# A hybrid decoder step on one core: four changes of order, among them a third pair of the second feed-forward in plain products

## The chip, the cores and the metric

The kernel runs on one core of a Trainium2 chip. The metric is the device time of one execution in microseconds (us); three runs of the kernel before have a median of 1526.13 us (1524.22 to 1526.34). Lower is better. In the text PE is TensorE, DVE is VectorE, ACT is ScalarE, POOL is GpSimd, SP is SyncE.

## The reference

One layer of a decoder, for 512 prompt tokens with 16 meta tokens ahead of them, and for 32 new tokens of 8 running sequences (560 columns in all, of which the last stages keep 544). The width is 1024, the feed-forward is 2816 wide.

```python
h = x + 0.5 * rms_norm(swiglu(rms_norm(x, ffn1_pre_g), ffn1_w_gate, ffn1_w_up, ffn1_w_down), ffn1_post_g)
u = rms_norm(h, mix_pre_g)
proj = u @ w_in
...
m = jax.nn.sigmoid(gate_a) * (o_a @ w_o_gla) + jax.nn.sigmoid(gate_b) * (o_b @ w_o_sb)
h = h + rms_norm(m @ w_out, mix_post_g)
y = h + 0.5 * rms_norm(swiglu(rms_norm(h, ffn2_pre_g), ffn2_w_gate, ffn2_w_up, ffn2_w_down), ffn2_post_g)
```

with `swiglu(x, g, u, d) = (silu(x @ g) * (x @ u)) @ d`. Between `proj` and `m` lie a gated linear attention (with a decay from a rank-16 projection, `w_gk2`), and a stick-breaking attention over the prompt and over cached pages.

## The kernel before, in words

All activations lie transposed: 128 features on the partitions, tokens along the free axis. Every matrix product is made of three products at a reduced float format (`float32r`): a weight and an activation are each split into a high part (a cast, on ACT) and a low part (value less high part, on DVE), and high x high, high x low and low x high are added in PSUM. One k-tile of one tile of 128 outputs is thus three matmuls for each half of the columns.

The program issues PE, DVE, ACT and POOL in an order that is written out by hand. A loop of matmuls calls `step()` after each k-tile (in the paired products after every two). Work of the other engines is put on a list with `later(n, f)`: f is issued n steps on, at that place of its engine's queue. Some stages have a table of their own besides (`when(n, f)`, n counted in steps of the stage). Each queue runs in order: an operation that waits holds up all that stand behind it. Loads are issued by SP, in order as well; weights land in three buffers (`raw`), and the next load of weights is issued when the low part of an earlier one has been made and its buffer is free.

Four places matter here.

**Gate rows.** In the pass over the value tiles of the mixer, `ranks` (the rank-16 projection) is followed by `ranks_end`, which writes its high and low parts in three row groups with `stack` (L216 to L223: a copy on ACT, two operations on DVE). `gla_gates` (L300s) then puts the pieces of head 0 on the list: `Gates.ranks` (two matmuls at L288 and two activations at L289), logs, sums and exponentials.

**Gates of the mixer.** The list `MIXER` gives the order in which output gates and output products are made: "R" is a plain product of eight k-tiles, "S" a pair of tiles made at once by `seven_steps` (L921 to L923), with seven products of half size where plain ones take eight (a form of Strassen's scheme). Such a pair needs sums of activations. They are made early, stored in DRAM (`sums_dram`) and come back by `sums_back` at the steps of `SUMS_BACK`, two loads (L2082) for each of four indices. Eight and ten steps later `sums_hi` casts them on ACT (L2088), two steps behind each of these `sums_lo` makes the low parts on DVE (L152 is the line of a helper that records every DVE `tensor_tensor`). The first pair begins at step 120 of this stage. In `seven_steps` the accumulator c takes a first product, is read by DVE (`v`, the sum of e5 and c), and then takes its last one.

**Output product.** `m @ w_out` runs tile by tile, for the first half of the columns (n = 0 to 7), then for the second. Its activations are `ms`, eight k-tiles, each made by `mixed` (L2250s) from a product `product_b`: the gate times the product, plus the other branch, then the cast (L2259) and the low part. The eighth is made from the product just ahead. `nm.tile` squares and scales each finished tile (L735, L736).

**Second feed-forward.** `early_tiles` makes the first three pairs of gate and up tiles; `other_tiles` makes the others by a plan, one letter for a pair: "R" is `eight` (L1081 to L1084: 96 matmuls, two tiles of eight k-tiles), "S" is `seven` (L1141 to L1143: 84 matmuls). The first "R" reads the normalised activations of `early_tiles` and 280 and 264 columns; from the second on the scaled copies `ub` are read, 272 and 272. `scaled_h`, `scaled_hi` and `scaled_lo` make `ub` (L1001 is the cast); `summed`, `sums_hi` (L1022) and `sums_lo` make the sums for the seven-product pairs, from the step `SP0` and again `SPE` steps later, (SP0, SPE) = `SUM2`. An "R" takes 16 steps of this stage and an "S" 14. The weights of the second and third plain pair are split by `parted` (the cast at L852) at 5 and at 1 step ahead of their tile; for a seven-product pair `weight_sums` (DVE) begins 10 steps ahead. The first feed-forward runs the same function with `PLAN1`, `SUM1` and 280 columns a half.

Of the kernel before, what the change touches and what calls it, by code (L numbers as in the profile page):

```python
# [17 lines left out]
KD = D // P  # L18
# [12 lines left out]


PLAN1 = "RRRSSSSSSSSSSSSSSSS"
PLAN2 = "RRSSSSSSSSSSSSSSSSS"
LATE1, LATE2 = 8, 8
SUM1, SUM2 = (14, 16), (4, 11)
UP1 = (2, 5)
UP2 = (2, 5)
RE_FFN = 3
U_SUMS = (5, 6, 9)  # L40
KEEP = 5
SUMS_BACK = (80, 86, 92, 106)
MIXER = [("R", "r", n) for n in range(3, 8)]
MIXER += [("R", "o", n) for n in range(8)] + [("R", "a", 0), ("R", "a", 1), ("S", "b", 0), ("S", "a", 2), ("S", "b", 2), ("R", "p", 0), ("R", "p", 1)]
MIXER += [("S", "a", 4), ("R", "p", 2), ("R", "p", 3), ("S", "b", 4), ("S", "a", 6), ("R", "p", 4), ("R", "p", 5), ("S", "b", 6)]
# [75 lines left out]
def hybrid_step(  # L121
# [25 lines left out]
    def ps(tag="ps"):  # L147
        count[0] += 1
        return pp.tile([P, 512], F32, tag=tag, name=f"{tag}{count[0]}")
# [58 lines left out]
    g_mix, g_mixpost, g_pre2 = gains[:, 8:16], gains[:, 16:24], gains[:, 24:32]  # L208
# [37 lines left out]
    W2 = (HW, W1)  # L246
# [68 lines left out]
    def gla_gates(hd, at, by):  # L315
        g = Gates(hd)
        for n, f in enumerate((g.ranks, g.logs, g.sums, g.exps)):
            later(at + by[n], f)
# [366 lines left out]
    def k_steps(acc, parts, k0, k1, kt, act, halves, nw=P, wid=(HW, HW)):  # L685
        hi, lo = parts
        for k in range(k0, k1):
            a = {h: act.get(k, h, wid[h]) for h in halves}
            wh, wl = hi[k - k0], lo[k - k0]
            for h in halves:  # L690
                T.matmul(acc[h][:nw, : wid[h]], wh, a[h][0], start=(k == 0), stop=False)  # L691
                T.matmul(acc[h][:nw, : wid[h]], wh, a[h][1], start=False, stop=False)  # L692
            for h in halves:
                T.matmul(acc[h][:nw, : wid[h]], wl, a[h][0], start=False, stop=(k == kt - 1))  # L694
            step()
# [17 lines left out]
    def later(n, f):  # L713
        todo.append([n, f])
# [498 lines left out]
    st.todo += [(w_out[0], 0, KD, P * n, P, n < 7 and "tile") for n in range(8)]  # L1213
    gate_up_weights(PLAN2, ffn2_w_gate[0], ffn2_w_up[0], 0)
    st.todo += [(ffn2_w_down[0], CUTS[j][0] * P, (CUTS[j][1] - CUTS[j][0]), P * n, P, False) for n, hs, j in by_chunks(DOWN) if (n, hs) != (7, (1,))]
    E = mybir.EngineType
    with tc.manual_schedule(engines={E.PE, E.DVE, E.Activation, E.Pool}):
# [217 lines left out]
        for h in range(2):  # L1435
            ranks(h)
            if h == 0:
                later(LATE[0], lambda: ranks_end(0))
            else:
                later(LATE[1], lambda: ranks_end(1))  # L1440
                gla_gates(0, 24, (0, 4, 7, 13))
                for k in range(KD):
                    later(MIX[0] + MIX[1] * k, lambda k=k: mix_tile(0, k))
                    later(32 + MIX[1] * k, lambda k=k: mix_tile(1, k))
                later(32 + MIX[1] * KD, mix_lo)
            for n in range(6):
                if h == 0:
                    vparts[n] = st.parts.pop(0)
                if h == 0 and n < 5 or h and n in (2, 4):
                    st.split()  # L1450
                    st.fetch()
                if n % 2 == 0:
                    vacc = [{h: ps("acc")} for _ in range(2)]
                for e in range(2):
                    value_chunk(n, e, vacc[e])
                if h and n > 1:
                    give(*vheld[n - 2])
        for n in (6, 7):
            vparts[n] = st.parts.pop(0)
        for e in range(2):  # L1460
            acc = {h: ps("acc") for h in range(2)}
# [14 lines left out]
        for j in range(5):  # L1476
            n = P if j < 4 else NTL
# [32 lines left out]
        for hd, head in enumerate(HEADS):  # L1510
# [10 lines left out]
            for c in range(2):  # L1521
# [3 lines left out]
                while True:  # L1525
                    try:
                        next(g)
                    except StopIteration as e:
                        acc = e.value
# [266 lines left out]
    for c in range(2):  # L1796
        t = cp.tile([P, 16], I32, name=f"idx{c}")
# [220 lines left out]
    def ahead():  # L2018
        st.split()
        st.fetch()  # L2020
# [118 lines left out]
    with tc.manual_schedule(engines={E.PE, E.DVE, E.Activation, E.Pool}):  # L2139
        kps = {}  # L2140
        for pr in range(9):
# [67 lines left out]
            n = 0  # L2209
# [33 lines left out]
        n = 8 * len(PAGES)  # L2243
# [3 lines left out]
        ms, msp = Parts(), {}  # L2247
# [27 lines left out]
        starts, n = {}, 0  # L2275
# [11 lines left out]
        for i in range(4):  # L2287
            when(SUMS_BACK[i], sums_back, i)
            for m in range(2):
# [20 lines left out]
        n = 0  # L2310
# [14 lines left out]
        def product(act, hs, parts):  # L2325
            acc = {h: ps("acc") for h in hs}
            k_steps(acc, parts, 0, KD, KD, act, hs, wid=W2)
            return acc
# [1 line left out]
        u2, rs2 = Parts(), take(NT)  # L2330
        n2 = Gain(u2, g_pre2, rs2, W2)

        nm, held = Norm(g_mixpost, W2), {}
        for i, (n, h) in enumerate([(n, 0) for n in range(8)] + [(n, 1) for n in range(7, -1, -1)]):
            if h == 0 or i % 2:
                ahead()
            if h == 0:
                held[n] = st.parts.pop(0)
            acc = product(ms, (h,), held[n])
            if h and n < 7:  # L2340
                give(*st.rooms[n])
            later(1, lambda n=n, h=h, acc=acc: nm.tile(n, h, acc[h]))
            if (n, h) == (7, 0):
                later(2, exp_ln_table)
            if (n, h) in ((7, 0), (0, 1)):
                for k in range(KD):
                    give(*ms.t[k, h])
                todo.extend([d, f] for d, f in n2.pieces(nm, h, *F1))
        del st.rooms[:7]
        hid, pairs = Parts(), {}  # L2350
        feed2 = other_tiles(u2, g_pre2, rs2, NW, W2, hid, pairs, PLAN2, LATE2, SUM2, UP2)
        early_tiles(u2, rs2, W2, NW, hid, pairs, {(0, 0): 9, (1, 0): 9}, lambda: next(feed2))
# [76 lines left out]
```

## Time and profile before

| | us |
|---|---|
| runs shown, median (lowest to highest) | 1526.13 (1524.22 to 1526.34) |
| the profiled execution | 1520.3 |
| its span, first to last instruction | 1518.6 |
| PE busy | 1499.9 |
| DVE busy | 1044.4 |
| ACT busy | 760.8 |
| mean granted TensorE clock | 0.996 |

The page is of one execution. Its first part gives the time in which each engine ran at least one instruction. A matmul's row lasts about 290 ns, since it counts from its start to its modelled end; the next one starts well before that. In a timeline each row gives the start and the duration in us, the engine, the line, the operation, what it writes and reads, the shapes, how many instructions were merged, and in brackets the idle time of the engine ahead of it with what ended that. In a table of stretches each engine has its busy time and its number of instructions, and the granted clock stands behind.

### The profile page before, as it was taken

What the parts mean: (1) busy time and instruction counts of PE and PEld (TensorE: products, weight loads), DVE (VectorE), ACT (ScalarE), POOL (GpSimd) and SP (SyncE); (2) the same over time, 40 slices, a digit from 0 to 9 for tenths busy, and PEclk for the clock granted to TensorE, in tenths of its full rate; (3) what the DMA queues carried; (4) which work ended last, traced back from release to release, by engine and by line L of the source; (5) the groups of instructions that cost most, each with busy time, mean ns of one, the idle gap of its engine ahead of it and who ended that gap; (6) DMA issues with size and microseconds to landing.
All of it is one profiled execution on the core that took longest, in us unless ns stands there. A gap on an engine that the chain in (4) does not pass through costs nothing.

```text
span 1518.6 us, 29559 instructions
## 1 busy us (share of the span) xinstructions
PE 1499.9 (99%) x11939; PEld 1446.4 (95%) x11939; DVE 1044.4 (69%) x1833; ACT 760.8 (50%) x1396; POOL 150.1 (10%) x216
## 2 busy tenths in 40 slices
PE   8999999999999999999999999999999999999998
PEld 8999999999999889999888999999999999999997
DVE  5788888523777766877776544987577998885234
ACT  6455454424665556566555443534465555444234
POOL 3000000000000111123324551000000000000000
PEclk9999999999999999999999999999999999999999
DMA  7133334524555473334555668335531344333343
GB/s 229 62 98 97 99 97 124 156 78 127 161 136 155 115 112 87 86 81 117 130 104 132 194 197 198 97 100 148 148 115 44 98 120 126 101 116 102 87 116 98
DMA packets 279577, 181.84 MB, mean 120 GB/s; under 512 B 10170, under 2 KB 264432, under 8 KB 279440
## 3 DMA queue, kind: packets, MB, share of 16 engines
q1 hardware_dynamic: 274000, 163.09, 40.5%
q0 software_dynamic: 5440, 16.85, 3.1%
q8 instruction: 94, 1.54, 0.4%
q14 instruction: 43, 0.35, 0.1%
HBM read 157.17 MB, written 22.74 MB: 118 GB/s over the span
## 4 chain that ended last, share of the span: by engine, by line
PE 91%; DVE 4%; ACT 3%; DMA 1%; issue 1%; SPq 0%; DVEq 0%; ACTq 0%
PE acc L691 9%; PE acc L692 9%; PE acc L694 9%; PE acc L1143 8%; PE acc L1141 8%; PE acc L1142 8%; PE acc L678 8%; PE acc L679 7%; PE acc L681 7%; DVE room L152 2%; PE ps L1763 1%; PE acc L921 1%; PE acc L923 1%; PE acc L922 1%; PE ps L1747 1%; PE acc L1084 1%
## 5 line engine op out<-in xcount | busy, mean ns | idle before, releaser
L152 DVE TENSOR_TENSOR lo<-raw,hi 128x1024 fp32r<-128x1024 f32 (+1 forms) x216 | 258.3, 1196 | 169.8 <-ACT hi L657 162.8
L152 DVE TENSOR_TENSOR room<-room,room 128x544 fp32r<-128x544 f32 (+17 forms) x369 | 238.9, 668 | 126.9 <-ACT room L735 57.6
L678 PE MATMUL acc<-room,hi 128*128 128x280 f32 (+1 forms) x928 | 271.7, 310 | 0.1
L1141 PE MATMUL acc<-room,hi 128*128 128x272 f32 (+1 forms) x924 | 267.7, 290 | 0.0
L1143 PE MATMUL acc<-room,lo 128*128 128x272 f32 (+1 forms) x924 | 267.5, 289 | 0.0
L1142 PE MATMUL acc<-room,hi 128*128 128x272 f32 (+1 forms) x924 | 267.5, 289 | 0.0
L679 PE MATMUL acc<-room,hi 128*128 128x280 f32 (+1 forms) x928 | 250.7, 289 | 0.0
L691 PE MATMUL acc<-room,hi 128*128 128x280 f32 (+1 forms) x784 | 221.8, 292 | 0.0
L692 PE MATMUL acc<-room,hi 128*128 128x280 f32 (+1 forms) x784 | 219.0, 289 | 0.0
L657 ACT CAST hi<-raw 128x1024 fp32r<-128x1024 f32 (+1 forms) x130 | 131.8, 1014 | 143.4 <-PE acc L692 124.9
L681 PE MATMUL acc<-room,lo 128*128 128x280 f32 (+1 forms) x928 | 192.6, 289 | 0.0
L694 PE MATMUL acc<-room,lo 128*128 128x280 f32 (+1 forms) x784 | 192.4, 290 | 0.0
L678 PEld LDWEIGHTS acc<-room,hi 128*128 128x128 f32 x928 | 174.9, 188 | 12.6 <-issue 10.7
L679 PEld LDWEIGHTS acc<-room,hi 128*128 128x128 f32 x928 | 175.1, 189 | 2.8 <-issue 1.9
L1143 PEld LDWEIGHTS acc<-room,lo 128*128 128x128 f32 x924 | 173.9, 188 | 0.0
L1141 PEld LDWEIGHTS acc<-room,hi 128*128 128x128 f32 x924 | 173.9, 188 | 0.0
L1142 PEld LDWEIGHTS acc<-room,hi 128*128 128x128 f32 x924 | 173.8, 188 | 0.0
L691 PEld LDWEIGHTS acc<-room,hi 128*128 128x128 f32 x784 | 147.6, 188 | 2.2 <-issue 0.9
L692 PEld LDWEIGHTS acc<-room,hi 128*128 128x128 f32 x784 | 147.5, 188 | 0.2
L852 ACT CAST hi<-raw 128x1024 fp32r<-128x1024 f32 x86 | 90.2, 1053 | 109.5 <-PE acc L1142 51.7
L681 PEld LDWEIGHTS acc<-room,lo 128*128 128x128 f32 x928 | 145.0, 188 | 0.0
L694 PEld LDWEIGHTS acc<-room,lo 128*128 128x128 f32 x784 | 133.9, 188 | 0.0
(354 smaller groups left out, 2831.4 us busy)
## 6 DMA issues: line engine op xcount, KB each, us to landing
raw<-in_w_in_dram SPq DMA_DIRECT2D x49, 512.0 KB, 8.5
raw<-in_ffn_w_down_dram SPq DMA_DIRECT2D x42, 448.0 KB, 3.8
raw<-in_ffn_w_gate_dram SPq DMA_DIRECT2D x66, 256.0 KB, 3.0
raw<-in_ffn_w_up_dram SPq DMA_DIRECT2D x66, 256.0 KB, 3.1
raw<-in_ffn_w_down_dram SPq DMA_DIRECT2D x21, 512.0 KB, 4.1
out_dram<-room SPq DMA_DIRECT2D x32, 256.0 KB, 3.0
raw<-in_w_in_dram SPq DMA_DIRECT2D x28, 256.0 KB, 4.4
h_dram<-room SPq DMA_DIRECT2D x24, 280.0 KB, 3.4
```

Of the source, the lines that this page charges most:

```text
L152: (eng or V).tensor_tensor(out=out, in0=a, in1=b, op=op)
L657: S.copy(h_, src)
L678: T.matmul(acc[h][:, : wid[h]], hi[k], a[h][0], start=(k == 0), stop=False)
L679: T.matmul(acc[h][:, : wid[h]], hi[k], a[h][1], start=False, stop=False)
L681: T.matmul(acc[h][:, : wid[h]], lo[k], a[h][0], start=False, stop=(k == KD - 1))
L691: T.matmul(acc[h][:nw, : wid[h]], wh, a[h][0], start=(k == 0), stop=False)
L692: T.matmul(acc[h][:nw, : wid[h]], wh, a[h][1], start=False, stop=False)
L694: T.matmul(acc[h][:nw, : wid[h]], wl, a[h][0], start=False, stop=(k == kt - 1))
L852: S.copy(hi[:, :kt], src)
L1141: T.matmul(x[:, :QW], hi, act[k][0], start=(first and k == 0), stop=False, skip_group_check=True)
L1142: T.matmul(x[:, :QW], hi, act[k][1], start=False, stop=False, skip_group_check=True)
L1143: T.matmul(x[:, :QW], lo, act[k][0], start=False, stop=(k == 3), skip_group_check=True)
```

## The change

Four edits. `PLAN2` makes the third pair of `other_tiles` in the second feed-forward a plain one ("R" for "S") and `SUM2` puts its sums at steps 14 and 30 where they stood at 4 and 15, so that the second plan and its sums are those of the first. The last entry of `SUMS_BACK` goes from 106 to 102. The pieces of the gate of head 0 begin 27 steps behind the ranks, not 24. And the output product makes seven k-tiles of tile 0, seven of tile 1, and then the eighth of both; `nm.tile` of both follows there.

```diff
-PLAN2 = "RRSSSSSSSSSSSSSSSSS"
+PLAN2 = "RRRSSSSSSSSSSSSSSSS"
 LATE1, LATE2 = 8, 8
-SUM1, SUM2 = (14, 16), (4, 11)
+SUM1, SUM2 = (14, 16), (14, 16)
...
-SUMS_BACK = (80, 86, 92, 106)
+SUMS_BACK = (80, 86, 92, 102)
...
-                gla_gates(0, 24, (0, 4, 7, 13))
+                gla_gates(0, 27, (0, 4, 7, 13))
...
-        nm, held = Norm(g_mixpost, W2), {}
+        nm, held, begun_ = Norm(g_mixpost, W2), {}, {}
         for i, (n, h) in enumerate([(n, 0) for n in range(8)] + [(n, 1) for n in range(7, -1, -1)]):
             if h == 0 or i % 2:
                 ahead()
             if h == 0:
                 held[n] = st.parts.pop(0)
+            if h == 0 and n < 2:
+                begun_[n] = {0: ps("acc")}
+                k_steps(begun_[n], held[n], 0, KD - 1, KD, ms, (0,), wid=W2)
+                if n:
+                    for m, acc in begun_.items():
+                        k_steps(acc, [t[KD - 1 :] for t in held[m]], KD - 1, KD, KD, ms, (0,), wid=W2)
+                        later(1, lambda m=m, acc=acc: nm.tile(m, 0, acc[0]))
+                continue
             acc = product(ms, (h,), held[n])
```

ACT's queue in the second feed-forward, where the weights of its second pair are cast: before. L852 casts the weights (`hi` from `raw`), L1022 the sums, L1088 is the activation of the first plain pair.

```order
L1001 COPY room_64_10597<-room_81_13221 128x544
L835 COPY room_36_3329<-room_40_5185 128x544
L1022 COPY room_78_12783<-room_82_13254 128x544
L1022 COPY room_68_11084<-room_82_13254 128x544
L1088 ACTIVATE room_80_13122<-room_80_13122 128x544
L1022 COPY room_84_13318<-room_83_13255 128x544 x2
L852 COPY hi_13322<-raw_12786 128x1024
L852 COPY hi_13357<-raw_13142 128x1024
```

The same place of ACT's queue in the change:

```order
L1001 COPY room_58_8967<-room_83_13222 128x544
L835 COPY room_37_4493<-room_33_962 128x544
L1088 ACTIVATE room_82_13173<-room_82_13173 128x544
L852 COPY hi_13311<-raw_12788 128x1024
L852 COPY hi_13344<-raw_13143 128x1024
L835 COPY room_58_8967<-room_82_13173 128x544
L1022 COPY room_80_12785<-room_84_13336 128x544
L1022 COPY room_78_12569<-room_84_13336 128x544
```

Four casts of sums stood ahead of the two weight casts and now stand behind them. On DVE, six operations for the sums (four of `summed`, two low parts) stood ahead of the weight's low part and stand behind it.

DVE's queue ahead of the first seven-product pair of the gates, before. The first row is the last of the weight sums, `room_40_5185` times `room_67` is a gate times its product, `lo` is a weight's low part, the rows that write `room_37` and `room_20` are the low parts of the last sums, L1994 copies small pieces of the sampled tokens.

```order
L152 TENSOR_TENSOR room_44_5335<-raw_10662,room_44_5335 128x512
L152 TENSOR_TENSOR room_40_5185<-room_67_10774,room_40_5185 128x544
L152 TENSOR_TENSOR lo_10803<-raw_10578,hi_10802 128x1024
L152 TENSOR_TENSOR room_37_4493<-room_33_962,room_66_10680 128x544
L1994 COPY room_40_5185<-ps_10813 64x32 x2
L1994 COPY room_43_5306<-ps_10813 64x32 x2
L1994 COPY room_5_70<-ps_10813 64x32 x2
L1994 COPY room_38_4495<-ps_10813 64x32 x2
L152 TENSOR_TENSOR room_20_260<-room_33_962,room_20_260 128x544
```

And in the change:

```order
L152 TENSOR_TENSOR room_44_5335<-raw_10662,room_44_5335 128x512
L152 TENSOR_TENSOR room_37_4493<-room_40_5185,room_66_10680 128x544
L152 TENSOR_TENSOR room_20_260<-room_33_962,room_20_260 128x544
L152 TENSOR_TENSOR room_40_5185<-room_67_10775,room_40_5185 128x544
L152 TENSOR_TENSOR lo_10806<-raw_10578,hi_10805 128x1024
L1994 COPY room_40_5185<-ps_10816 64x32 x2
```

The two low parts went ahead of the gate's product and of the weight's low part.

PE's queue in the output product, before, from the seventh k-tile of tile 0 (`acc_12261`) to the first of tile 1 (`acc_12299`). `room_31_874` holds the eighth k-tile of `ms`.

```order
L691 MATMUL acc_12261<-room_62_10030,room_63_10527 128x280
L692 MATMUL acc_12261<-room_63_10527 128x280
L694 MATMUL acc_12261<-room_62_10030,room_64_10597 128x280
L691 MATMUL acc_12261<-room_31_874,room_63_10527 128x280
L692 MATMUL acc_12261<-room_31_874,room_63_10527 128x280
L694 MATMUL acc_12261<-room_31_874,room_64_10597 128x280
L691 MATMUL acc_12299<-room_70_11346,room_64_10597 128x280
```

In the change, from the seventh k-tile of tile 1 (`acc_12297`) to the end of both; the eighth k-tile is in `room_14_144`, and tile 0 is `acc_12262`.

```order
L691 MATMUL acc_12297<-room_62_10030,room_66_10680 128x280
L692 MATMUL acc_12297<-room_64_10597,room_66_10680 128x280
L694 MATMUL acc_12297<-room_62_10030,room_66_10680 128x280
L691 MATMUL acc_12262<-room_14_144,room_64_10597 128x280
L692 MATMUL acc_12262<-room_14_144,room_64_10597 128x280
L694 MATMUL acc_12262<-room_14_144,room_65_10612 128x280
L691 MATMUL acc_12297<-room_14_144,room_66_10680 128x280
```

The 21 matmuls of tile 1's first seven k-tiles now stand ahead of the first matmul that reads the eighth.

## The prediction, made before the changed kernel ran

> **What bounds the kernel now.** I read the page first, then the waits of TensorE, then the timeline and the stretches around the four places that the change touches. The page's span and busy lines come first:
>
> ```profile
> span 1518.6 us, 29559 instructions
> PE 1499.9 (99%) x11939; PEld 1446.4 (95%) x11939; DVE 1044.4 (69%) x1833; ACT 760.8 (50%) x1396; POOL 150.1 (10%) x216
> ```
>
> TensorE (PE) is busy for 99% of the span. A change can gain only by fewer matmuls or by shorter pauses of PE. The two longest waits of PE at one place, with total, times and longest:
>
> ```profile
> PE ps L2364 <- DVE room L152: 3.2, 1, 3.2
> PE acc L1081 <- ACT hi L852: 2.3, 1, 2.3
> ```
>
> The first is the kernel's tail, which the change leaves alone. The second is in the second feed-forward, one of the four seams. To price a pause I need what a matmul costs in the stream, which is not its own duration (about 290 ns, since matmuls overlap) but its pitch. Three stretches of PE; the columns are us, busy time (instructions), granted clock, DMA share, GB/s:
>
> ```profile
> 1175.00:1177.50 2.50, 0.21 (x2) 1.00 0.00 0
> 1177.50:1181.00 3.50, 3.23 (x12) 0.51 0.19 45
> 1210.00:1360.00 150.00, 150.00 (x1199) 1.00 0.38 112
> ```
>
> The third stretch is the steady second feed-forward: 150 us over 1199 matmuls, **0.125 us a matmul**. The second is the cost that the wait list does not show: behind the pause the granted clock is 0.51, and 12 matmuls take 3.46 us (from 1177.54 to 1181.00) where 1.50 would do. All losses below are start to start, less 0.125 for each matmul.
>
> **Seam 1, gate rows three steps later.** PE, then DVE, before:
>
> ```profile
> 440.91 0.29 PE L288 MATMUL ps<-room,wgk 128*128 128x280 f32 x1
> 442.01 0.37 PE L288 MATMUL ps<-room,wgk 128*128 128x280 f32 x1 [0.81 <-DVE room L221]
> 442.22 0.29 PE L691 MATMUL acc<-room,room 128*128 128x280 f32 x1
> ```
> ```profile
> 441.57 0.30 DVE L221 CAST room<-room 16x280 fp32r<-16x280 f32 x1
> ```
>
> The two gate matmuls take 1.31 us from 440.91 to 442.22 instead of 0.25: **1.06 lost**. The second waits for the copy that ends at 441.87. The change puts nine value matmuls ahead of the pair, 9 x 0.125 = 1.13, so the second is due at 440.91 + 1.13 + 0.13 = 442.17, 0.3 behind the copy. What the step issues besides (two activations, one DVE operation, later the logs, sums and exponentials) goes back by three steps too: the exponentials come at step 40 of the 64 that this pass of value tiles still has, ahead of the first head. I cost that at nothing. If the cover of 0.3 is gone, the price is what is missing of it.
>
> **Seam 2, the last sums loaded four steps earlier.** PE's two pauses, in the first and the second seven-product pair of the gates:
>
> ```profile
> 959.69 0.29 PE L923 MATMUL acc<-room,lo 128*128 128x272 f32 x1
> 960.82 0.39 PE L921 MATMUL acc<-room,hi 128*128 128x272 f32 x1 [0.84 <-DVE room L152]
> 961.05 0.28 PE L922 MATMUL acc<-room,hi 128*128 128x272 f32 x1
> ```
> ```profile
> 971.29 0.29 PE L923 MATMUL acc<-room,lo 128*128 128x272 f32 x1
> 971.77 0.39 PE L921 MATMUL acc<-room,hi 128*128 128x272 f32 x1 [0.19 <-DVE room L152]
> 972.00 0.29 PE L922 MATMUL acc<-room,hi 128*128 128x272 f32 x1
> ```
>
> The first loses 1.36 - 0.25 = 1.11, the second 0.71 - 0.25 = 0.46. What PE waits for is not a sum but DVE's addition `v`, which must read the accumulator before the last product adds to it. DVE runs through from 946.59 to there:
>
> ```profile
> 945.16 0.73 DVE L152 TENSOR_TENSOR room<-room,room 128x544 f32<-128x544 f32 x1 [1.49 <-ACT room L2050]
> 946.59 1.23 DVE L152 TENSOR_TENSOR lo<-raw,hi 128x1024 fp32r<-128x1024 f32 x1 [0.70 <-ACT hi L852]
> ```
> ```profile
> 960.34 0.43 DVE L152 TENSOR_TENSOR room<-room,acc 128x272 f32<-128x272 f32 x1
> ```
>
> The change moves the two low parts of the last sums out of this queue, ahead of the row at 945.16, into its idle 1.49. Each is one 128x544 operation at 0.65 (five in 3.25, in the row at 1174.60 below). So `v` ends 1.3 earlier, at 959.47, and PE wants it at 959.69 + 0.125 = 959.81: the first pause closes by 0.3. In the second pair PE comes 1.11 earlier, and wants its `v` at 971.29 + 0.125 - 1.11 = 970.30; DVE gives it at 971.71 - 1.3 = 970.41. I leave 0.2 there: **gain 1.11 + 0.26 = 1.37**. The loads themselves move past the two quarter loads of the next weights on SyncE's queue:
>
> ```profile
> 928.03 2.65 SPq L2082 DMA_DIRECT2D room<-sums_dram  x1
> 932.90 1.35 SPq L617 DMA_DIRECT2D raw<-in_w_in_dram  x2
> ```
>
> The queue stood empty from 930.68 to 932.90, when the weights' buffer came free; the second load of sums takes this place, so I let the weights land as before. Were they late, DVE's weight sums would be late by as much, and the gain would go first.
>
> **Seam 3, the first two output tiles end with their eighth k-tile.**
>
> ```profile
> 1076.81 0.29 PE L694 MATMUL acc<-room,room 128*128 128x280 f32 x1
> 1077.67 0.40 PE L691 MATMUL acc<-room,room 128*128 128x280 f32 x1 [0.56 <-ACT room L2259]
> 1078.83 0.40 PE L692 MATMUL acc<-room,room 128*128 128x280 f32 x1 [0.76 <-DVE room L152]
> 1079.07 0.29 PE L694 MATMUL acc<-room,room 128*128 128x280 f32 x1
> ```
> ```profile
> 1078.06 0.72 DVE L152 TENSOR_TENSOR room<-room,room 128x544 fp32r<-128x544 f32 x1
> ```
>
> Three matmuls take 2.26: **1.88 lost** to the last mixer tile, whose low part is ready at 1078.78. The change puts 21 matmuls of tile 1 (2.63 us) ahead: the low part is wanted at 1076.94 + 2.63 + 0.125 = 1079.69, 0.9 behind. No matmul is added. The squares and scalings of tile 0 come eight steps later, beside those of tile 1: four ACT operations of 0.4 to 0.5 in a row, behind which weight splits for tiles 4 and on stand; PE comes to tile 4 only after tiles 2 and 3, 48 matmuls or 6 us. Of four accumulators two are open for longer, and tile 4 is the first to ask for one of them again, behind the same 6 us. I cost that at nothing.
>
> **Seam 4, the third pair plain and the sums from step 14.** PE, ACT and DVE where the second pair begins:
>
> ```profile
> 1174.93 0.28 PE L1084 MATMUL acc<-room,lo 128*128 128x264 f32 x1
> 1177.54 0.59 PE L1081 MATMUL acc<-room,hi 128*128 128x272 f32 x1 [2.33 <-ACT hi L852]
> ```
> ```profile
> 1173.38 1.20 ACT L1022 CAST room<-room 128x544 fp32r<-128x544 f32 x2 [1.26 <-DVE room L152]
> 1174.49 0.66 ACT L1088 ACTIVATE room<-room 128x544 f32<-128x544 f32 x1
> 1175.35 1.19 ACT L1022 CAST room<-room 128x544 fp32r<-128x544 f32 x2 [0.21 <-DVE room L152]
> 1176.45 1.99 ACT L852 CAST hi<-raw 128x1024 fp32r<-128x1024 f32 x2
> ```
> ```profile
> 1174.60 3.25 DVE L152 TENSOR_TENSOR room<-room,room 128x544 f32<-128x544 f32 x5
> 1177.78 1.21 DVE L152 TENSOR_TENSOR lo<-raw,hi 128x1024 fp32r<-128x1024 f32 x1
> ```
>
> PE would have begun at 1175.05 and begins at 1177.54: 2.49 lost, and 3.46 - 1.50 = 1.96 more at the halved clock, **4.45 in all**. The weight's high part (L852) stands behind the sums' casts (L1022), which wait for DVE's sums. The order puts six sum operations of DVE and four casts behind it. DVE's low part then ends 6 x 0.65 = 3.9 earlier, at 1178.99 - 3.9 = 1175.1; the fifth matmul wants it at 1175.05 + 0.5 = 1175.55, so 0.45 is left. On ACT the activation at 1174.49 has three sums less ahead of its DVE input, 1.95, and one pair of casts: it begins near 1172.2, and L852 gives its first weight near 1173.9. The pause closes and with it the slow stretch.
>
> The price is the plain pair: 96 matmuls for 84, 12 x 0.125 = **1.50**, nothing beside it. It also saves DVE and ACT the third pair's weight sums. The next wait could come where the first seven-product pair now begins, 192 matmuls or 24 us after 1175.05, with all sums to be done: 16 sum operations at 0.65, five weight low parts at 1.14 (1177.78 to the next start), four weight sums near 0.7 and five small ones, near 22 us. So 2 us of cover; without it the price is a pause like today's, 0 to 4.45. I take 0, because the first feed-forward runs this very table:
>
> ```profile
> 72.60 0.29 PE L1084 MATMUL acc<-room,lo 128*128 128x280 f32 x1
> ```
> ```profile
> 71.02 1.22 DVE L152 TENSOR_TENSOR lo<-raw,hi 128x1024 fp32r<-128x1024 f32 x1
> ```
> ```profile
> 97.20:270.20 173.00, 173.00 (x1342) 1.00 0.37 107
> ```
>
> There the low part ends at 72.24, 0.36 ahead of its matmul, and the 16 seven-product pairs run without a pause.
>
> **The sum**: 1.06 + 1.37 + 1.88 + 4.45 - 1.50 = 7.26, say 7.3 us. The profiled execution took 1520.3, its span 1518.6; it would take 1513.0. The runs shown have a median of 1526.13, 5.8 above it; I carry the gain over unchanged: **1518.8 us**.
>
> A rule to weigh: the half clock follows a pause of 2.49 us here (rows above). [...]
>
> **The rivals.**
> - The half clock is no part of the usual execution. For it: one trace shows it, and the pauses of 0.9 to 1.0 us in the other seams have no such stretch behind them, so the limit lies somewhere between 1.0 and 2.49. Then the 1.96 were never lost: 7.3 - 2.0 = 5.3, **1520.8**.
> - The wait of seam 4 comes back, at its own place or at the first seven-product pair, long enough to halve the clock. For it: DVE has 2 us to spare in 24. Against it: the first feed-forward. Price up to 4.45: **1523.3**.
> - A seam does not do what it says: seam 2's loads delay the weights behind them, or `v` stays late. Its 1.37 goes: **1520.2**.
> - Slower: the shift by one pair puts the weight loads of the 16 seven-product pairs out of step with their three buffers, and each waits a little. From 0.65 us a pair it decides: 16 x 0.65 = 10.4 eats 7.3 and 3.1 more, **1529.2**. Against it: the first feed-forward's 173 us with the same rotation, all busy.
>
> **How the numbers follow.** The forecast 0.60, the clock rival 0.15, the returned wait 0.13, seam 2 alone 0.07, slower 0.05. A change under 0.2%, 3.05 us, cannot be told from none. Forecast, clock rival and seam 2 lie beyond it; the returned wait at 2.9 lies on its edge and is mostly counted as the same. Faster 0.83, same 0.12, slower 0.05. The range takes the forecast, the clock rival and seam 2, with the runs' own spread of 2 us (1524.22 to 1526.34) halved to each side, and a part of the returned wait: 1517.2 to 1522.6.
>
> **What would show it.** Right: no idle time ahead of the second L288; none ahead of L921 in the first gate pair, at most 0.2 in the second; none in the first two output tiles; at the second pair of the second feed-forward no gap, and a granted clock of 1.00 in the stretch that now shows 0.51; 12 more matmuls of L1081 to L1143. Wrong: a new gap ahead of L1141 in the first seven-product pair, a gap ahead of L1084 behind the weight's low part, or small ones in every pair.

## The result and the profile after

The changed kernel takes **1518.2 us** (median of 6 runs, 1517.38 to 1519.75) against 1526.14 for the kernel before (6 runs, 1524.22 to 1527.28): a ratio of 0.9947 (95% interval 0.9937 to 0.9957), 7.9 us less. A second comparison, in another session, gave 1514.62 against 1522.27, ratio 0.9953 (0.9939 to 0.9966), 7.65 us less. The forecast was 1518.8, 7.3 less.

The page of the changed kernel, its span and busy lines:

```profile
span 1515.9 us, 29553 instructions
PE 1500.3 (99%) x11951; PEld 1447.1 (95%) x11951; DVE 1039.2 (69%) x1823; ACT 758.3 (50%) x1392; POOL 151.2 (10%) x216
```

PE has the 12 matmuls more (11951 for 11939). The span is only 2.7 us below that of the first profile of before, though the runs gained 7.9. The longest waits of PE after the change, with total, times and longest, show both why the seams are closed and where the profiled execution lost something else:

```profile
PE ps L2372 <- DVE room L152: 3.2, 1, 3.2
PE ps L1958 <- issue: 2.2, 4, 1.0
PE ps L1303 <- DVE room L1302: 1.7, 1, 1.7
```

None of L288, L921, L691, L692 and L1081 is left with a wait on a row of its seam. New is L1958, the short matmuls of the sampled tokens, ahead of which PE stood without a releaser:

```profile
846.71 0.44 PE L1958 MATMUL ps<-room,room 128*32 128x128 f32 x5 [0.21 <-issue]
848.12 0.47 PE L1958 MATMUL ps<-room,room 128*32 128x128 f32 x8 [0.98 <-issue]
```

The seams themselves. PE and ACT at the second pair of the second feed-forward:

```profile
1174.66 0.42 PE L1084 MATMUL acc<-room,lo 128*128 128x280 f32 x2
1174.91 0.28 PE L1081 MATMUL acc<-room,hi 128*128 128x272 f32 x1
```
```profile
1172.08 0.66 ACT L1088 ACTIVATE room<-room 128x544 f32<-128x544 f32 x1 [0.69 <-DVE room L152]
1172.64 1.99 ACT L852 CAST hi<-raw 128x1024 fp32r<-128x1024 f32 x2
```

The weight casts stand at 1172.64 where they stood at 1176.45, and the second pair follows the first at the pitch of the stream (0.25 us for the two matmuls from 1174.66 to 1174.91). DVE's low part of the same weight, and the stretch behind it, whose granted clock (the first figure behind the five engines) was 0.51 before:

```profile
1173.86 1.22 DVE L152 TENSOR_TENSOR lo<-raw,hi 128x1024 fp32r<-128x1024 f32 x1
```
```profile
1174.90:1178.40 3.50, 3.50 (x30) 3.50 (x29) 3.50 (x7) 0.65 (x1) 0.00 (x0) 1.00 0.51 148
```

The low part ends at 1175.08, 0.3 ahead of the first matmul that reads it (1175.40), and the granted clock is 1.00 (the 0.51 behind it is the DMA share). The eighth k-tile in the output product, and the one place that did not close fully, the second seven-product pair of the gates:

```profile
1078.46 0.29 PE L694 MATMUL acc<-room,room 128*128 128x280 f32 x1
1078.59 0.29 PE L691 MATMUL acc<-room,room 128*128 128x280 f32 x1
1078.72 0.29 PE L692 MATMUL acc<-room,room 128*128 128x280 f32 x1
```
```profile
973.25 0.29 PE L923 MATMUL acc<-room,lo 128*128 128x272 f32 x1
973.46 0.39 PE L921 MATMUL acc<-room,hi 128*128 128x272 f32 x1
973.69 0.28 PE L922 MATMUL acc<-room,hi 128*128 128x272 f32 x1
```

973.25 to 973.69 is 0.44 for two matmuls, 0.19 more than their pitch: the 0.2 that the prediction left there.

To compare traces place by place I set equal matmuls of two traces beside each other and read how their distance grows. The table gives that growth, in us against the first profile of before (minus is a gain); the last column is the time from the first L1081 of the second feed-forward's other pairs to their last L1143.

| kernel | first 60 us | gate rows, 430 to 470 | sampled tokens, 840 to 900 | gates, 950 to 1000 | output product, 1070 to 1095 | other pairs |
|---|---|---|---|---|---|---|
| before, first profile | 0 | 0 | 0 | 0 | 0 | 207.33 |
| changed, first profile | +0.07 | -1.19 | **+4.04** | -1.37 | -1.81 | 204.16 |
| changed, again | +1.90 | -1.19 | 0.00 | -1.27 | -1.81 | 204.16 |
| before, again | +2.09 | 0.00 | 0.00 | +0.12 | 0.00 | 209.13 |
| before, third | -0.34 | 0.00 | 0.00 | -0.05 | 0.00 | 207.38 |
| second feed-forward alone | +1.75 | 0.00 | 0.00 | +0.01 | +0.01 | 204.10 |
| three seams | +0.69 | -1.19 | 0.00 | -1.30 | -1.81 | 207.93 |

In the first profiles the seams gain 1.19 + 1.37 + 1.81 + 3.17 = 7.54, and 4.04 of it is lost at L1958; that leaves 3.5, of which the rest of the program takes 0.8 by the end of the span.

### The profile page after: what moved, and what is told of

It reads as the page before. It is cut to its first block, busy times and chain, and to the rows that moved or that the text cites. A ratio compares the mean times of both kernels' runs of the same rounds, so it can differ in the third digit from the quotient of the medians.

```text
span 1515.9 us, 29553 instructions
## 1 busy us (share of the span) xinstructions
PE 1500.3 (99%) x11951; PEld 1447.1 (95%) x11951; DVE 1039.2 (69%) x1823; ACT 758.3 (50%) x1392; POOL 151.2 (10%) x216
## 4 chain that ended last, share of the span: by engine, by line
PE 96%; ACT 2%; DVE 1%; issue 0%; ACTq 0%
PE acc L691 10%; PE acc L694 10%; PE acc L692 10%; PE acc L678 8%; PE acc L1143 8%; PE acc L1142 8%; PE acc L1141 8%; PE acc L679 7%; PE acc L681 7%; PE acc L921 2%; PE acc L1081 2%; PE acc L923 2%; PE acc L922 2%; PE acc L1082 2%; PE acc L1084 2%; PE ps L1763 1%
## 5 line engine op out<-in xcount | busy, mean ns | idle before, releaser
L678 PE MATMUL acc<-room,hi 128*128 128x280 f32 (+1 forms) x928 | 271.8, 310 | 0.1
L1141 PE MATMUL acc<-room,hi 128*128 128x280 f32 (+1 forms) x896 | 259.5, 290 | 0.0
L1142 PE MATMUL acc<-room,hi 128*128 128x280 f32 (+1 forms) x896 | 259.4, 290 | 0.0
L1143 PE MATMUL acc<-room,lo 128*128 128x280 f32 (+1 forms) x896 | 259.4, 290 | 0.0
L679 PE MATMUL acc<-room,hi 128*128 128x280 f32 (+1 forms) x928 | 250.7, 289 | 0.0
L691 PE MATMUL acc<-room,hi 128*128 128x280 f32 (+1 forms) x784 | 221.7, 292 | 0.0
L692 PE MATMUL acc<-room,hi 128*128 128x280 f32 (+1 forms) x784 | 219.0, 290 | 0.0
L681 PE MATMUL acc<-room,lo 128*128 128x280 f32 (+1 forms) x928 | 192.7, 289 | 0.0
L694 PE MATMUL acc<-room,lo 128*128 128x280 f32 (+1 forms) x784 | 192.3, 290 | 0.0
L678 PEld LDWEIGHTS acc<-room,hi 128*128 128x128 f32 x928 | 174.8, 188 | 12.8 <-issue 10.7
L679 PEld LDWEIGHTS acc<-room,hi 128*128 128x128 f32 x928 | 175.1, 189 | 2.7 <-issue 1.9
L1143 PEld LDWEIGHTS acc<-room,lo 128*128 128x128 f32 x896 | 168.6, 188 | 0.0
L1141 PEld LDWEIGHTS acc<-room,hi 128*128 128x128 f32 x896 | 168.5, 188 | 0.0
L1142 PEld LDWEIGHTS acc<-room,hi 128*128 128x128 f32 x896 | 168.5, 188 | 0.0
L691 PEld LDWEIGHTS acc<-room,hi 128*128 128x128 f32 x784 | 147.5, 188 | 2.0 <-issue 0.9
L692 PEld LDWEIGHTS acc<-room,hi 128*128 128x128 f32 x784 | 147.5, 188 | 0.2
L681 PEld LDWEIGHTS acc<-room,lo 128*128 128x128 f32 x928 | 145.0, 188 | 0.0
L852 ACT CAST hi<-raw 128x1024 fp32r<-128x1024 f32 x86 | 90.1, 1052 | 107.6 <-PE acc L1142 47.0
L694 PEld LDWEIGHTS acc<-room,lo 128*128 128x128 f32 x784 | 134.1, 188 | 0.0
```

The lines of the kernel that those rows point to most:

```text
L678: T.matmul(acc[h][:, : wid[h]], hi[k], a[h][0], start=(k == 0), stop=False)
L679: T.matmul(acc[h][:, : wid[h]], hi[k], a[h][1], start=False, stop=False)
L681: T.matmul(acc[h][:, : wid[h]], lo[k], a[h][0], start=False, stop=(k == KD - 1))
L852: S.copy(hi[:, :kt], src)
L1141: T.matmul(x[:, :QW], hi, act[k][0], start=(first and k == 0), stop=False, skip_group_check=True)
L1142: T.matmul(x[:, :QW], hi, act[k][1], start=False, stop=False, skip_group_check=True)
```

## The experiments

**The kernel before, profiled again** (no edit).

> The kernel before, unchanged, profiled again. The profile of the changed kernel has idle time of PE in the bursts of short matmuls of the sampled tokens (L1958) that the first profile of before has not: from the shift of equal matmuls between the two traces, -1.03 us at 838 and +2.97 us at 898, so 4.0 us. Theory A: such pauses are part of the usual execution of both kernels, and the first profile of before is one without them, which is why it lies 5.8 us below the median of its runs. Then this profile shows about 4 us (2 to 6) of idle time at L1958 and a time of 1523 to 1527. Theory B: the pauses come from the change; then this profile has none at L1958, and a time near 1520. Against the kernel before: ratio 1.000.

Measured: ratio 0.9995 (0.9986 to 1.0004), median 1522.11, the profiled execution 1524.37. Theory A falls: nothing is idle at L1958. What this execution has over the first one is 2.1 us in the first 60 us and 1.8 us in the second feed-forward. Theory B, that the change makes the pauses, stays open here.

**The second feed-forward alone.**

```diff
-PLAN2 = "RRSSSSSSSSSSSSSSSSS"
+PLAN2 = "RRRSSSSSSSSSSSSSSSS"
-SUM1, SUM2 = (14, 16), (4, 11)
+SUM1, SUM2 = (14, 16), (14, 16)
```

> Only the edit of the second feed-forward (third pair plain, sums from step 14). Theory A (the half clock behind the pause is part of the usual execution): 4.45 - 1.50 = 2.95 us less, ratio 0.9981. Rival (half clock only in the profiled execution): 0.99 us less, ratio 0.9994. In the profile: no pause ahead of the second pair, granted clock 1.00 behind it; the three other seams as before (1.06, 1.57 and 1.88 us).

**The three other seams**: the changed kernel with these two lines as before.

> The changed kernel with the second feed-forward as before: gate rows, sums and output tiles alone. Theory A: 1.06 + 1.37 + 1.88 = 4.3 us less, ratio 0.9972; the pause of 2.3 us ahead of the second pair and the half clock stay. Rival (the gain in the timed runs comes from somewhere else than the seams): a ratio within 0.0007 of 1.

Measured: the first alone 0.9978 (0.9969 to 0.9987), 3.3 us less (0.0022 x 1522.4); the others 0.9981 (0.9971 to 0.9991), 2.9 us less. The forecasts of Theory A, 2.95 and 4.3, lie in these intervals, the second at the edge of its own; its trace gains 1.19 + 1.30 + 1.81 = 4.30 at the three seams. Both rivals lie outside. Each edit accounts for its own seams and no other. The waits of PE between 430 and 1480 show it; the edit of the second feed-forward alone leaves

```profile
PE acc L921 <- DVE room L152: 1.1, 2, 0.8
PE ps L288 <- DVE room L221: 0.8, 1, 0.8
PE acc L692 <- DVE room L152: 0.8, 1, 0.8
PE acc L691 <- ACT room L2259: 0.6, 1, 0.6
```

and the three others leave

```profile
PE acc L1081 <- ACT hi L852: 2.4, 1, 2.4
PE acc L1084 <- DVE lo L152: 0.7, 1, 0.7
```

The rest of both lists is equal. The runs give 3.3 + 2.9 = 6.2 for the parts, the whole 7.65 to 7.9; the intervals of the parts are 1.4 us to each side, so they don't contradict it.

**The plain pair without the later sums** (only the `PLAN2` line).

> Only the plain third pair, with the sums at their old steps 4 and 15. Theory A (the pause is made by the place of the sums in the queues of ACT and DVE): the pause of 2.3 us and the half clock stay, and 12 matmuls more cost 1.5 us: ratio 1.0010. Rival (the plain pair itself makes the room): the pause goes, 2.95 us less, ratio 0.9981.

Measured: 1.0011 (1.0002 to 1.0020), 1.7 us more. Theory A: the wait of 2.3 us on L852 stays, and the 12 matmuls cost what they cost. In this execution the granted clock behind the wait was 1.00, and the other pairs took 207.98, 0.65 more than in the first profile of before, where the 12 matmuls alone make 1.50: 0.85 of the old price was missing.

**The changed kernel, profiled again** (no edit).

> The changed kernel, unchanged, profiled again. The profile of the three seams alone, which has the same program up to the second feed-forward, showed no pause at L1958, so Theory A' (the 4.0 us of pauses there belong to that one execution, not to the change): no idle time at L1958 here, and in the trace, place by place against the first profile of before: -1.19 at the gate rows, -1.35 in the gates, -1.81 in the output product, -2.9 in the second feed-forward. Against the kernel before 7.3 to 8 us less, ratio 0.9950. Rival (the change brings the pauses): about 4 us of idle time at L1958 again, ratio 0.9950 + 0.0026 = 0.9976.

Measured: 0.9953 (0.9939 to 0.9966). No row of L1958 has idle time, as Theory A' expected, and each seam repeats its gain within 0.1 us (table). So the change doesn't bring the pauses by itself; of all the profiles here they are in one alone.

**The bursts at L1958 cut in two.**

```diff
-                when(8 * i + 1, use_values, c, b0)
+                when(8 * i + 1, use_values, c, b0, 0)
+                when(8 * i + 3, use_values, c, b0, 1)
```

> The changed kernel with each burst of short matmuls at L1958 cut in two halves, two steps apart. If PE is held there because too many short instructions stand behind each other, and this is usual: up to 4 us less than the changed kernel, ratio to before 0.9924. If the pauses belong to single executions (Theory A'): the time of the changed kernel, ratio to before 0.9950, and no idle time at L1958.

Measured: 0.9967 (0.9955 to 0.9979), 2 us above the changed kernel, which neither theory expected. The trace says why: beside the changed kernel profiled again, it loses 1.33 us between 840 and 900 and 1.37 between 900 and 950, eight cuts in 2.7 us, **0.34 us for each**. One whole burst, with the stream on both sides, and one half of a cut one:

| | from the last matmul ahead to the first behind |
|---|---|
| 32 of L1958, changed kernel | 1.22 us |
| 16 of L1958, this run | 0.78 to 0.79 us |

Going from the large matmuls to these of 32 columns (`128*32` in the rows) and back has a price of its own here, the 0.34 us of a cut; the matmuls themselves cost (1.22 - 0.785) / 16 = 0.027 us each.

**Half of two doses**: gate rows from 25, last sums at 104.

```diff
-SUMS_BACK = (80, 86, 92, 102)
+SUMS_BACK = (80, 86, 92, 104)
-                gla_gates(0, 27, (0, 4, 7, 13))
+                gla_gates(0, 25, (0, 4, 7, 13))
```

> The changed kernel with half of two doses: gate rows from step 25 (not 27) and the last sums at 104 (not 102). Theory A: each step of the gate rows puts three matmuls, 0.375 us, ahead of the pair, so the one step gains 0.38 of 1.06 and an idle time of about 0.45 stays ahead of the second L288. At 104 one low part of 0.65 stands ahead of DVE's saturated stretch and the other behind it, so the gates gain 0.65, and pauses of 0.46 stay in both of the first two seven-product pairs. Rival (the gain is not in proportion, the steps 27 and 102 were needed because something else had to be passed): no gain at one place or the whole gain there.

There is one run (1516.28 us), too little to compare times. Measured, in the trace: the gates gain 0.65, as expected, but unevenly (0.2 stays in the first pair, 0.5 in the second). At the gate rows the idle time ahead of the second L288 is 0.42, as expected, and yet nothing is gained by 470:

```profile
442.43 0.37 PE L288 MATMUL ps<-room,wgk 128*128 128x280 f32 x1 [0.42 <-DVE room L221]
452.21 0.40 PE L691 MATMUL acc<-room,hi 128*128 128x280 f32 x1 [0.26 <-ACT room L1433]
```

The 0.38 is given back 10 us on, where PE waits for ACT's copy of an accumulator (L1433), which ends at 452.16:

```profile
450.50 0.43 ACT L1358 CAST room<-room 128x280 fp32r<-128x280 f32 x1 [2.89 <-DVE room L155]
450.83 1.05 ACT L657 CAST hi<-raw 128x1024 fp32r<-128x1024 f32 x1
451.78 0.38 ACT L1433 COPY room<-acc 128x280 f32<-128x280 f32 x1
```

The cast L1358 at the head of this row stood idle for 2.89 until DVE's L155, which with step 25 stands behind the gate's scan (L300):

```profile
447.81 1.32 DVE L300 TENSOR_TENSOR_SCAN room<-room,room 128x560 f32<-128x560 f32 x1
449.17 0.88 DVE L152 TENSOR_TENSOR room<-room 128x512 f32<-128x512 f32 x3
449.96 0.50 DVE L155 SCALAR_TENSOR_TENSOR room<-room,gains,room 128x280 f32<-128x280 f32 x1
```

The kernel before has the same order and the same 2.89 of idle time there; its copy ended at 451.75, and PE went on at 451.80. In the changed kernel, profiled again (its first 60 us took 1.5 us longer), the scan comes behind that operation, and the copy L1433 has run 1.2 us before:

```profile
448.10 0.51 DVE L155 SCALAR_TENSOR_TENSOR room<-room,gains,room 128x280 f32<-128x280 f32 x1
448.53 0.45 DVE L152 TENSOR_TENSOR room<-room,room 128x280 fp32r<-128x280 f32 x1
449.48 0.74 DVE L155 SCALAR_TENSOR_TENSOR room<-room 128x560 f32<-128x560 f32 x1 [0.51 <-ACT room L294]
450.26 1.32 DVE L300 TENSOR_TENSOR_SCAN room<-room,room 128x560 f32<-128x560 f32 x1
```
```profile
450.62 0.38 ACT L1433 COPY room<-acc 128x280 f32<-128x280 f32 x1
```

The rival holds at this place: one step is not enough, because the scan has to go behind that operation as well. Step 26 was not run.

**The sums on POOL.** The changed kernel with the plan of before (sums from 4 and 15, third pair of seven products), its eight sum operations on POOL.

```diff
-            tt(*((s1, a21, a22, ALU.add), (s3, a11, a21, ALU.subtract), (s2, s1, a11, ALU.subtract), (s4, a12, s2, ALU.subtract))[n])
+            tt(*((s1, a21, a22, ALU.add), (s3, a11, a21, ALU.subtract), (s2, s1, a11, ALU.subtract), (s4, a12, s2, ALU.subtract))[n], eng=G if nw < NT else V)
```

> The changed kernel with the second plan as before (third pair of seven products, sums from step 4 and 15), but with the eight sum operations of the second feed-forward on POOL, which has nothing to do there. Theory A (the pause is DVE's lack of time: eight operations of 0.65 us are 5.2 us in a stretch where DVE runs through): the pause ahead of the second pair goes without the price of the plain pair, 1.46 us under the changed kernel, ratio to before 0.9940. Rival (POOL's operation is much longer than 0.65 us, four of them stand in a chain, and ACT's casts wait for them ahead of the weight's cast, or POOL slows DVE): the pause stays or moves to the third pair, ratio to before 0.9965 or more.

Measured: 1.0015 (1.0006 to 1.0024), 9.4 us above the changed kernel ((1.0015 - 0.9953) x 1522.3); the other pairs take 213.85. The rival holds. POOL, then DVE:

```profile
1174.44 1.75 POOL L152 TENSOR_TENSOR room<-room,room 128x544 f32<-128x544 f32 x1 [8.59 <-DVE room L152]
1176.15 1.83 POOL L152 TENSOR_TENSOR room<-room 128x544 f32<-128x544 f32 x1
```
```profile
1173.65 6.69 DVE L152 TENSOR_TENSOR room<-room,room 128x544 fp32r<-128x544 f32 x5
1180.26 2.35 DVE L152 TENSOR_TENSOR lo<-raw,hi 128x1024 fp32r<-128x1024 f32 x1
```

One operation takes POOL 1.75 to 1.84 in four rows of one, and 3.37 in a fifth (the first of the eight, from 1157.06). The five of DVE in the row above are two that started ahead of POOL's first, at 0.72 each, and three beside POOL (from 1174.91, 1176.70 and 1178.49) at 1.85 to 1.87; each of the three ends 0.58 to 0.59 behind the POOL operation that ran when it started, and a weight's low part takes 2.35 instead of 1.2. PE then waited 2.61 ahead of L1081 and 5.08 ahead of L1084, and the clock was halved for 6.83 us. Why DVE's operations are longer beside POOL's is not shown. One that reads an accumulator was not longer: 0.42 at 1164.56, beside POOL's from 1162.19 to 1165.86, and 0.42 at 1163.41 in the first profile of before, where POOL does nothing.

**Sums at other steps, third pair of seven products**: the changed kernel with `PLAN2` as before, and `SUM2` (9, 9) or, in a second run, (12, 7).

```diff
-PLAN2 = "RRRSSSSSSSSSSSSSSSS"
+PLAN2 = "RRSSSSSSSSSSSSSSSSS"
-SUM1, SUM2 = (14, 16), (14, 16)
+SUM1, SUM2 = (14, 16), (9, 9)
```

> The changed kernel with the third pair of seven products again, but the sums at steps 9 and 18, so that half of them stand behind the weights of the second pair. Theory A (only the place of the sums counts; they have slack at the third pair): no pause ahead of the second pair and none later, 1.5 us under the changed kernel, ratio to before 0.9940. Rival (DVE runs through from 1159 to 1199 in the trace of before and has no time left; the plain pair is what gives it): the pause comes back inside or ahead of the third pair, 1 to 3 us with a half clock behind it, ratio to before 0.9955 to 0.9975.

> As the run with steps 9 and 18, with the sums at 12 and 19: the first group is wholly behind the weights' casts, the second stands one step closer to the third pair, which begins at step 32. Theory A: no pause, ratio to before 0.9940, as with 9 and 18. Rival (DVE has no time): a longer wait than there at the third pair, ratio to before 0.9960 to 0.9980.

Measured: 0.9967 (0.9955 to 0.9978) and 0.9980 (0.9971 to 0.9989), other pairs 206.28 and 208.58. The rival holds in both: the waits move. The half clock that the rival expected followed only in the second, for 3.41 us behind the wait of 2.4. Waits of PE from 1160 to 1200, first with 9 and 18, then with 12 and 19:

```profile
PE acc L1084 <- DVE lo L152: 1.5, 1, 1.5
PE acc L1143 <- DVE lo L152: 0.7, 1, 0.7
PE acc L1141 <- ACT hi L852: 0.6, 1, 0.6
```
```profile
PE acc L1141 <- ACT hi L852: 2.4, 1, 2.4
PE acc L1143 <- DVE lo L152: 0.7, 1, 0.7
PE acc L1084 <- DVE lo L152: 0.2, 1, 0.2
```

L1141 and L1143 are the third pair. With the sums later PE waits less at the second pair and more at the third, 2.8 and 3.3 us in sum. (With 9 and 18 the gates gained only 0.76, with the same code there; why is open.)

**The kernel before, a third time** (no edit).

> The kernel before once more, for two things. The pause ahead of the second pair of the second feed-forward has cost 4.43, 6.23 and 5.07 us where the third pair had seven products, and 3.58 with a plain one, by half clocks of one, two, one and no window of 3.41 us. If the windows run free of the program, this one lies at one of the same steps (no, one or two windows: 3.6, 4.4 to 5.1, or 6.2 us). And if the pauses of 4.0 us at L1958 belong to a chip and not to the change, they appear here where the kernel before has a median near 1526, and are missing where it has one near 1522.

Measured: 1.0001 (0.9992 to 1.0010). No pause at L1958, and a median of 1521.88. No half clock behind the pause; but the other pairs take 207.38, as in the first profile, which had 3.4 us of it. Waits from 1160 to 1200:

```profile
PE acc L1081 <- ACT hi L852: 2.3, 1, 2.3
PE acc L1084 <- DVE lo L152: 0.7, 1, 0.7
PE acc L1143 <- DVE lo L152: 0.6, 1, 0.6
```

In the first profile the second of these was 0.2 and the third was not there.

**Without the low parts of the sums**: the kernel with sums at 9 and 18, which leaves out eight of DVE's operations.

```diff
                 hi, lo = sp_[i, m, k]
-                tt(lo[:, :nw], pairs_of(sr_[i, m])[:, k], hi[:, :nw].bitcast(F32), ALU.subtract)
+                if nw < NT:
+                    lo = hi
+                else:
+                    tt(lo[:, :nw], pairs_of(sr_[i, m])[:, k], hi[:, :nw].bitcast(F32), ALU.subtract)
```

> The kernel of the run with seven products in the third pair and sums at 9 and 18, which leaves out the eight low parts of the sums in the second feed-forward (the high parts are read in their place): eight DVE operations of 0.65 us, 5.2 us, are gone, and nothing else moves. Theory B, the one that the runs so far favour (DVE has no time left between 1160 and 1200; its lateness is what PE waits for, wherever it shows): the waits of 1.65, 0.78 and 0.90 us in and around the second and third pair go, and without the plain pair's price this ends about 1.5 us under the changed kernel, ratio to before 0.9940. Rival (the waits there come from the weights' loads and their three buffers, or from ACT): they stay, 3.3 us in all, ratio to before near 0.9967.

Measured: 0.9952 (0.9938 to 0.9965), the time of the changed kernel, not 1.5 us less; other pairs 205.14. Two theories in one stretch: both waits of the third pair are gone, as Theory B has it, and the wait of 1.5 in the second pair stands as it stood, which it has not.

```profile
PE acc L1087 <- DVE lo L152: 1.5, 1, 1.5
```

(L1084 stands three lines lower here.) That wait is one of order: DVE makes the weight's low part behind sums of the first group, and these were not left out. DVE's lack of time was thus shown for the third pair, not for the second. Another 0.7 of the 205.14 stands in no single wait and stays open (204.16 - 1.50 is 202.66, and the wait with the matmuls beside it costs 1.74).

## Why the prediction was right

**Gate rows, 1.06.** Measured 1.19 in every trace with step 27: 1.04 at the pair, and 0.15 at the wait for L1433, 10 us on, which the forecast did not have. The second L288 was said to come 0.3 behind the copy: in the changed kernel, profiled again, the copy on DVE ends at 443.77 and the pair runs at 443.98. That the other pieces of the step cost nothing was right for 27, but by a margin that I had not looked at: as step 25 shows, that next wait takes a smaller gain back.

**Sums of the gates, 1.37.** Measured 1.37, 1.27 and 1.30 (1.20 to 1.44 in the other traces with the sums at 102, but 0.76 in one), with 0.19 left in the second pair where 0.2 was forecast. The loads ahead of the weights held nothing up.

**Output product, 1.88.** Measured 1.81 in every trace. The cost of the wider order was nothing, as said.

**Second feed-forward, 4.45 - 1.50 = 2.95.** Against the first profile of before 3.17 (207.33 to 204.16), and against the four traces with the old plan, 207.33, 209.13, 207.38 and 207.93 (mean 207.94), 3.8. The positions came out as worked out: the low part ends at 1175.08 (forecast 1175.1), and DVE had idle time left on the way to the first seven-product pair (1.63 us from 1185.37, where 2 us of cover were forecast). But the term for the half clock, 1.96, was **wrongly understood**. Waits for DVE's low parts stand behind the pause, and a slow PE hid part of them: in the three executions with half clock they were 0.2, 0.6 and 0.7 us, none at the third pair. Where the clock stayed full (before, third profile), they showed as 0.7 and 0.6 us, and the whole cost the same; where the half clock lasted two windows instead of one, it cost 1.8 more. So the rival "the half clock is no part of the usual execution" had its condition right (it was missing in two of five executions with this pause: the third of before and the plain pair alone) and its price wrong: with the old plan nothing was to be taken off, and with the plain pair, which has no wait in the third pair, 0.85. Nor is it a matter of the pause's length alone, with a limit between 1.0 and 2.49 us, as the rival had it: the same pause came with and without half clock (last section). That the 4.45 of one trace served is in part luck: the other three traces with the old plan would have given 6.25, 4.5 and 5.05.

**Carrying the gain from one execution to the runs.** The seams' 7.5 us stand in the runs as 7.65 and 7.9. But the difference of the two first profiles was 2.7, and it would have misled: the changed one had 4.04 us of pauses at L1958, and single executions differ by up to 2.4 us in their first 60 us (-0.34 to +2.09). That the first profile of before lay 5.8 below its runs was left unexplained. Part is now seen: its first 60 us were 2.1 shorter than in the second profile of before, and its other pairs 1.8. The rest goes with the session: the four later comparisons have medians of 1522.1 to 1522.6 for the kernel before, the first has 1526.1, and the changed kernel is 3.6 us slower there as well. The 1520.3 of the first profile is not among the six runs of the first comparison, and lies within the runs of the later ones (1519.82 to 1524.79). Pauses like those at L1958, in both kernels of that session, would make up this difference, and so would a slower chip: the four later comparisons ran on four chips, and that of the first is not on record. Neither is shown, since no profile of the kernel before is known to come from that session. What causes the pauses at L1958 stays open: cutting the bursts was no test, because no later execution had them.

The other rivals: the wait of seam 4 did not return with the plan of the change, and was shown to return where the third pair has seven products; no wait in the 16 seven-product pairs was seen.

## What to carry to other kernels

A wait whose releaser has no time left was not removed by moving it: sums moved behind the weight casts came back as waits one pair later (1.3 us with the sums at 9 and 18, 3.1 with 12 and 19), and only the later sums together with the plain pair, 1.5 us of matmuls that also spares DVE its weight sums, ended them (the plain pair alone left 2.3 us). Price a slow clock behind a pause together with the waits that it covers, not as a term beside them. And compare traces place by place, over equal instructions: the difference of two spans held one execution's accidents, 4 us in size, beside gains of 1 to 3.

## What the hardware showed that I had not expected

The pause of 2.3 us at the second pair was followed by half clock for 3.4, 6.8, 3.4, 0 and 0 us in five executions (before first, before again, three seams, plain pair alone, before third). Two of them, granted clock behind the busy times, the long one and one without:

```profile
1181.00:1187.00 6.00, 5.69 (x25) 5.69 (x26) 6.00 (x11) 1.35 (x3) 0.00 (x0) 0.50 0.32 93
```
```profile
1181.00:1187.00 6.00, 6.00 (x51) 6.00 (x50) 6.00 (x11) 2.58 (x5) 0.00 (x0) 1.00 0.54 155
```

25 matmuls in the one, 51 in the other, behind the same wait. The periods are whole multiples of 3.41 us (1177.54 to 1180.96, 1180.33 to 1187.16), and within one execution all changes of the clock lie on one grid of this step (in the first profile of before, 17.01 and 1177.55 are 340 steps apart), which begins elsewhere in each execution (a change to full clock stands at 17.01 there, at 17.44 in the first profile of the changed kernel). Laid over the pause, this grid tells the five apart:

| execution | window that the pause reaches | idle time of PE in it | matmuls begun in it | granted clock behind it |
|---|---|---|---|---|
| before, first profile | 1174.13 to 1177.55 | 2.33 | 8 | 0.50 |
| before, again | 1176.92 to 1180.33 | 2.32 | 7 | 0.50 |
| three seams | 1171.85 to 1175.27 | 2.65 | 4 | 0.50 |
| plain pair alone | 1174.31 to 1177.72, and the next | 1.55, 1.51 | 13, 13 | 1.00, 1.00 |
| before, third | 1173.11 to 1176.53, and the next | 1.58, 1.48 | 13, 13 | 1.00, 1.00 |

The pause brought half clock where nearly all of it fell into one window, and none where a boundary cut it in two. A window of the steady stream begins 27 matmuls (3.41 us at 0.125 each). Counted over the whole program in all 14 traces, every window at full clock with fewer than 10 matmuls begun was followed by half clock, none with 13 or more was, and with 10 to 12 both came. So whether this pause cost half clock depended on where it fell on the grid, and in three executions of one program (the kernel before) that came out twice one way and once the other. That the number of matmuls is what decides is read off these counts; no run varied it.

None of the windows ahead of half clock was idle throughout: in the table PE was busy for 0.77 to 1.09 us of each.

A change to matmuls of 32 columns and back cost 0.34 us on PE (eight cuts of bursts of 32 such matmuls, 2.7 us).
